# A first product that waits for two PSUM banks: a hybrid RWKV-7 and Conformer backbone on one core

## The chip, the core and the metric

The kernel runs on one NeuronCore of a Trainium2 chip. The metric is the device time in microseconds of one execution, the median of several runs. The engines meant below are TensorE (PE, with its weight loads as PEld), VectorE (DVE), ScalarE (ACT), GpSimd (POOL) and SyncE (SP), each with an instruction stream of its own. TensorE writes its products to PSUM banks of 128 x 512 fp32; ScalarE and VectorE read them from there.

## The reference, cut to what matters

A backbone of two layers over 512 latent tokens with a prefix of 256 context tokens and a width of 1024. The first layer runs a bidirectional RWKV-7 time mixing (16 heads of 64) beside a gated short convolution; the second is a Conformer convolution module. The change lies in the time mixing, whose core is this recurrence, run forwards and backwards:

```python
def wkv_scan(S0, r, decay, k, v, kk, a, reverse):
    def step(S, inp):
        r_t, w_t, k_t, v_t, kk_t, a_t = inp
        sa = jnp.einsum("bhvk,bhk->bhv", S, -kk_t)
        S = (S * w_t[:, :, None, :]
             + sa[..., None] * (kk_t * a_t)[:, :, None, :]
             + v_t[..., None] * k_t[:, :, None, :])
        return S, jnp.einsum("bhvk,bhk->bhv", S, r_t)
    S, out = lax.scan(step, S0, (r, decay, k, v, kk, a), reverse=reverse)
    return out, S
```

All of it is fp32. The context is scanned first from a zero state, and its final states start the scan of the latent tokens.

## The kernel before

The scan is done in chunks of 64 tokens, for one pair of heads (128 channels, 64 partitions for each head) at a time: 4 blocks of context (`c0` to `c3`), then 8 latent pairs, each of 8 chunks and two directions `z`. For each pair there are these steps, in functions of their own:

- `light0` and `lightz` (one call for each direction) make the decays and the scaled keys and queries, `AR` and `BK`. Each call of `lightz` makes two small dense products, `lw` and `la`, that ScalarE reads with a Tanh (lines 511 and 517).
- `heavy` makes what the recurrence needs from each chunk. For a latent pair its parts run in the order `A`, `N`, `B`, `V`. `pa` (A) forms the head products in four groups, each half of the chunks of one direction: 4 chunks times 2 heads, so 8 products of 64 rows, the heads on the two halves of the partitions. Head `h` writes to a bank of its own, `pas[h]`, and VectorE reads both with a masked multiplication into `E` (line 601), first head 0, then head 1. `pb` (B) transposes the keys in two groups, one for each direction, of 16 small transposes (line 576) into two banks `pbs[h]`, which ScalarE copies into `BKt` (line 612).
- `solve` inverts the small triangular systems on VectorE (lines 656 and 658), `merge` joins their blocks, and `chain_lat` runs the recurrence, chunk by chunk.

All these banks come from one tag, `at`, with two buffers. A product may write to a bank once the reader of what stood there before is done. In the code of `pa` and `pb` the products of a group alternate between the banks, head 1 first. `pinned()` returns a helper that ties each product of a group to the one before it, so that their order on TensorE is the written one.

What stands between the products of a group is left to a planner. It fixes the order of each engine's instructions when the program is built: among those whose inputs and buffers it expects to be ready, it takes the earliest by the written order, with some tied to later points by hand (`HEAVY_AFTER`, `CONV_AFTER`, `issue_after`). While the small products of a pair wait, it issues the dense products of 128 x 512 of the convolution branch and the gates (`pcg`, `pxb`, `pbg`, `pzb`, each 24 instructions, from `conv_branch`).

The stages of the latent pairs follow each other in the order of `STAGE[1]`: recurrence of pair s, then bonus product, solve for pair s + 1, loads and light part of pair s + 2, merge for pair s + 1, heavy part of pair s + 2, fills and finish, convolution branch. After the last pair come the output projection and the Conformer layer.

Of the kernel before, what the change touches and what calls it, by code (L numbers as in the profile page):

```python
# [10 lines left out]
AF = mybir.ActivationFunctionType  # L11
ALU = mybir.AluOpType
# [3 lines left out]
P = 128  # L16
# [6 lines left out]
CH = 64  # L23
NCTX = CTX // CH
NLAT = SEQ // CH
# [12 lines left out]
ZR = (slice(0, 64), slice(64, 128))  # L38
# [13 lines left out]
def kernel(ctx: ExitStack, tc: tile.TileContext, I: dict, out: bass.AP):  # L52
    nc = tc.nc
    V, S, G, T = nc.vector, nc.scalar, nc.gpsimd, nc.tensor
# [122 lines left out]
    def w(tag, name, dt=F32):  # L177
        return wk.tile([P, SIZE.get(tag, 512)], dt, tag=tag, name=name, bufs=NBUF.get(tag, 1))

    def ch3(t, x=CH):  # L180
        return t.rearrange("p (c x) -> p c x", x=x)

    def small(name, shape):
        return cvp.tile(shape, F32, tag=name, name=name)
# [7 lines left out]
    maskE = small("maskE", [P, 3, P])  # L192
    scm = small("scm", [P, NLAT * 66])
    sg = small("sg", [P, NLAT, 66])
# [12 lines left out]
    def hc(nmh, j):  # L207
        return hcol[:, half[nmh] + j : half[nmh] + j + 1]
# [297 lines left out]
    def lightz(st, z):  # L506
        lat, nm, parts, low, kk = (st[x] for x in ("lat", "nm", "parts", "low", "kk"))
        k_, r_, bon = st["k"], st.get("r"), st.get("bon")
        pl = low(0, z, f"lw{nm}{z}")
        for p, cs in parts:  # L510
            S.activation(sg[:, cs.start // CH : cs.stop // CH, 1:65], ch3(pl[:, cs]), AF.Tanh,
                         bias=hc("w0", z * 8 + p), scale=0.5)
        S.activation(sg[:, :, 1:65], sg[:, :, 1:65], AF.Identity, bias=ones)
        pl = low(1, z, f"la{nm}{z}")
        a = w("a", f"a{nm}{z}")
        for p, cs in parts:
            S.activation(a[:, cs], pl[:, cs], AF.Tanh, bias=hc("a0", z * 8 + p), scale=0.5)
        cumf = w("P", f"P{nm}{z}")
        cum = ch3(cumf, 66)
        sgf = sg.rearrange("p c x -> p (c x)")  # L520
        V.tensor_tensor_scan(cumf, scm, sgf if z == 0 else sgf[:, ::-1], 0.0, ALU.mult, ALU.add)
        iP = ch3(w("tmp", f"iP{nm}{z}"))
        S.activation(iP, cum[:, :, 1:65], AF.Exp, scale=0.5 * KAPPA)
        S.activation(cumf, cumf, AF.Exp, scale=-0.5 * KAPPA)
        PC = w(f"PC{z}", f"PC{nm}{z}")
        S.copy(PC, cum[:, :, 64])
        st["PC"].append(PC)
        kd = w("kd", f"kd{nm}{z}")
        for p, cs in parts:
            S.activation(kd[:, cs], a[:, cs], AF.Identity, scale=hka[:, p : p + 1], bias=oka[:, p : p + 1])  # L530
        V.tensor_tensor(out=kd, in0=kd, in1=k_, op=ALU.mult)
        if lat:
            p = st["p"]
            rk = col("r_k", 8 * z + p)
            if z:
                V.scalar_tensor_tensor(out=bon, in0=kd, scalar=rk, in1=bon, op0=ALU.mult, op1=ALU.add)
                V.tensor_tensor(out=bon, in0=bon, in1=r_, op=ALU.mult)
            else:
                S.activation(bon, kd, AF.Copy, scale=rk)
        V.scalar_tensor_tensor(out=a, in0=a, scalar=1.0, in1=kk, op0=ALU.add, op1=ALU.mult)  # L540
        AR = ch3(w("AR", f"AR{nm}{z}"), P)
        BK = ch3(w("BK", f"BK{nm}{z}"), 3 * CH)
        kka, ba, kdc, Pr, iPr = ch3(kk), ch3(a), ch3(kd), cum, iP
        if z:
            Pr, iPr = Pr[:, ::-1, :], iP[:, ::-1, :]
            kka, ba = kka[:, :, ::-1], ba[:, :, ::-1]
        if not lat:
            V.scalar_tensor_tensor(out=AR[:, :, 0:CH], in0=kka, scalar=-1.0, in1=Pr[:, :, 0:CH],
                                   op0=ALU.mult, op1=ALU.mult)
        else:  # L550
            V.scalar_tensor_tensor(out=AR[:, :, 0:CH], in0=kka, scalar=-1.0, in1=Pr[:, :, 0:CH],
                                   op0=ALU.mult, op1=ALU.mult)
            Pi = Pr[:, :, 1:65]
            V.tensor_tensor(out=AR[:, :, CH:], in0=ch3(r_), in1=Pi[:, :, ::-1] if z else Pi, op=ALU.mult)
        V.scalar_tensor_tensor(out=BK[:, :, ZR[1]], in0=ba, scalar=0.5, in1=iPr, op0=ALU.mult, op1=ALU.mult)
        V.tensor_tensor(out=BK[:, :, ZR[0]], in0=kdc, in1=iPr[:, :, ::-1] if z else iPr, op=ALU.mult)
        S.copy(BK[ZR[1], :, P:], BK[ZR[1], :, ZR[0]])
        st["AR"].append(AR)
        st["BK"].append(BK)

    def pinned():
        prev = []

        def go(o, lhsT, rhs, start=True, stop=True, op=mm):
            e = op(o, lhsT, rhs, start, stop)
            if prev:
                tc.add_manual_dep(e.ins, prev[-1].name,
                                  mybir.DependencyInfo(mybir.DependencyClass.NoSync, mybir.DependencyReason.DATA),
                                  reason="written order")
            prev[:] = [e.ins]  # L570
            return e

        return go
# [7 lines left out]
    def heavy(st, an=None):  # L581
        ha = (None,) * 4 if an is None else HEAVY_AFTER[an["lat"]]
        lat, nm = st["lat"], st["nm"]
        v_ = st["v"]
        UV = buf("UV", st)
        E = buf("E", st)
        st["UV"], st["E"], st["BKt"] = UV, E, [buf("BKt", st, z) for z in range(2)]

        def pa():
            for gi, (z, g) in enumerate(PA_ORDER if lat else ((0, 0), (1, 0))):  # L590
                with anchored(an, ha[gi if lat else 2 * gi]):
                    AR, BK = st["AR"][z], st["BK"][z]
                    m, x = (4, P) if lat else (8, CH)
                    c0 = m * g
                    pas = [ch3(ps_at(f"pa{nm}{z}{g}{h}"), x) for h in range(2)]
                    go = pinned()
                    for c in range(m):
                        for h in (1, 0):
                            go(pas[h][:, c, :], kb(BK, h, c0 + c), AR[ZR[h], c0 + c, 0:x])
                    for h in range(2):  # L600
                        V.tensor_tensor(out=E[:, h, z * NLAT + c0 : z * NLAT + c0 + m, :], in0=pas[h],  # L601
                                        in1=maskE[:, z * (1 + h) : z * (1 + h) + 1, 0:x].to_broadcast([P, m, x]), op=ALU.mult)

        def pb():
            for z in range(2):
                pbs = [ch3(ps_at(f"pb{nm}{z}{h}")) for h in range(2)]
                go = pinned()
                for c in range(NLAT):
                    for h in (1, 0):
                        go(pbs[h][:, c, :], kb(st["BK"][z], h, c), ident[ZR[h], ZR[h]], op=tr)  # L610
                for h in range(2):
                    S.copy(st["BKt"][z][:, :, ZR[h]], pbs[h])

        def nt():
            for h in range(2):
                for b in range(2):
                    rs = slice(64 * (1 - h) + 32 * b, 64 * (1 - h) + 32 * b + 32)
                    S.copy(Nt[rs], E[rs, h, :, 32 * b : 32 * b + 32])

        def pv():  # L620
            pv = ch3(ps_at(f"pv{nm}"))
            for c in range(NLAT):
                for h in range(2):
                    mm(pv[ZR[h], c, :], v_[ZR[h], c * CH : (c + 1) * CH], ctr[ZR[h], ZR[h]], True, True)
            for z in range(2):
                for h in range(2):
                    src = pv[ZR[h]].rearrange("p (j c) x -> p j c x", j=2)
                    dst = UV[ZR[h], z * NLAT : (z + 1) * NLAT, ZR[h]].rearrange("p (j c) x -> p j c x", j=2)
                    S.copy(dst, src if lat or not z else src[:, :, ::-1, :])

        def po():
            if lat:
                bon = st["bon"]
                pb = ps_at("pbon" + nm)
                mm(pb, blk, bon, True, True)
                V.scalar_tensor_tensor(out=bon, in0=pb, scalar=0.5, in1=v_, op0=ALU.mult, op1=ALU.mult)

        st["po"] = po
        for x in HEAVY[lat]:
            {"A": pa, "B": pb, "N": nt, "V": pv, "O": po}[x]()  # L640
# [278 lines left out]
    for s in range(12):  # L919
        st = sts[s]  # L920
# [9 lines left out]
        for x in STAGE[s >= 4]:  # L930
# [17 lines left out]
            elif x == "C":  # L948
                conv_branch(s - 3, st["anchor"])
                if s == 10:  # L950
                    rs.close()
                    op = rs.enter_context(tc.tile_pool(name="op", bufs=1, reuse_waits="tile", side="right"))
# [40 lines left out]
    with ExitStack() as l1:  # L993
# [118 lines left out]
        for n in range(4):  # L1112
            ws = {}
            for part, tag in ((1, "wa"), (0, "wb")):
                for kt in range(0, KT, 2):
                    c0 = part * EC + n * 512
# [6 lines left out]
            for m in range(4):  # L1123
# [10 lines left out]
                a = lt("a", f"a{n}{m}")  # L1134
# [31 lines left out]
        for j in range(16):  # L1166
            c0 = 2 * EC + j * P
# [138 lines left out]
```

## Time and profile before

| | us |
|---|---|
| median of three runs | 1466.74 |
| lowest and highest run | 1463.91, 1472.64 |
| span of the profiled execution | 1468.7 |
| TensorE busy in it | 1417.8 |
| VectorE busy | 987.8 |
| ScalarE busy | 749.9 |
| GpSimd busy | 128.4 |

The span is counted from the first to the last instruction of one execution that the profiler recorded; no other time is given for that execution. In the timeline a row gives the start and the length of an instruction, or of several of a kind that follow each other (x14), with the idle time before it and what ended it in brackets. Matmul lengths overlap, as they are pipelined, so distances from start to start are what counts. An fp32 product of the heads is two instructions, a transpose is one; a group of `pa` thus shows as 16 instructions `pal<-ARl,BKl` and a group of `pb` as 16 instructions `pbl<-ident,BKl`. The granted clock of TensorE was 0.978 of full speed on average over the span.

### The profile page before, as it was taken

Reading aid. Unit: us, or ns where it says so; the run is one execution under the profiler, and the core shown is the slowest. Engines: PE = TensorE matmul, PEld = TensorE weight load, DVE = VectorE, ACT = ScalarE, POOL = GpSimd, SP = SyncE. Lnnn points to the kernel's source line nnn. Section 1 sums busy time; section 2 is a strip of 40 time slices with the busy share of each in tenths; the row PEclk is TensorE's granted clock in tenths of the full one; section 3 lists DMA queues with packets and bytes.
Section 4 is the critical chain, followed back from the end, with each engine's and each line's share of the span. In section 5 each row is a group of like instructions: output and inputs, shape, how many; then the busy total and the mean of one; then the engine's idle time right before and its main releaser. Section 6 shows DMA issues by size and latency. Waiting matters only on the chain. (4 is left out here: it accounts for less than half of the span.)

```text
span 1468.7 us, 29754 instructions
## 1 busy us (share of the span) xinstructions
PE 1417.8 (97%) x11921; PEld 1014.3 (69%) x11921; DVE 987.8 (67%) x2298; ACT 749.9 (51%) x1516; POOL 128.4 (9%) x250
## 2 busy tenths in 40 slices
PE   6999999999999999999999999999989999999998
PEld 1564677878776766666666666777757777788876
DVE  2675587567798989898998988558535535544333
ACT  4536364353655575666656655447543423463222
POOL 2023210000110101101011000011100000000000
PEclk9999999979898999999999999999999999999999
DMA  9755433312232312222222222468503303123322
GB/s 318 221 169 165 151 112 94 99 40 76 75 91 80 97 54 87 64 80 66 68 86 77 61 68 70 169 227 295 177 16 115 104 12 115 58 88 100 100 87 86
DMA packets 137627, 158.55 MB, mean 108 GB/s; under 512 B 15375, under 2 KB 104143, under 8 KB 137369
## 3 DMA queue, kind: packets, MB, share of 16 engines
q1 hardware_dynamic: 121104, 106.47, 23.1%
q0 software_dynamic: 15312, 48.99, 10.2%
q8 instruction: 94, 1.54, 0.4%
q10 hardware_dynamic: 1072, 1.19, 0.3%
q14 instruction: 45, 0.37, 0.1%
HBM read 138.33 MB, written 18.28 MB: 107 GB/s over the span
## 5 line engine op out<-in xcount | busy, mean ns | idle before, releaser
L57 PE MATMUL o<-wh,y 128*128 128x512 f32 x248 | 80.5, 402 | 0.0
L656 DVE TENSOR_TENSOR xtmpl<-Xl,Yl 128x126 f32<-128x126 f32 (+22 forms) x248 | 62.1, 251 | 2.9
L658 DVE TENSOR_TENSOR Yl<-Yl,xtmpl 128x126 f32<-128x126 f32 (+22 forms) x248 | 62.0, 250 | 2.6
L57 PE MATMUL pal<-ARl,BKl 64*128 64x128 f32 x512 | 57.2, 301 | 3.5 <-DVE xtmpc L656 2.1
L57 PEld LDWEIGHTS pal<-ARl,BKl 64*128 64x128 f32 x512 | 42.1, 190 | 23.0 <-issue 5.4
L1141 ACT CAST ah<-a 64x512 fp32r<-64x512 f32 x32 | 19.8, 618 | 72.9 <-DVE a L1136 72.5
L57 PE MATMUL zol<-UV,E 64*64 64x64 f32 (+1 forms) x1024 | 54.0, 221 | 0.0
L57 PE MATMUL o<-wl,y 128*128 128x512 f32 x124 | 50.0, 403 | 4.0 <-DVE wl L127 4.0
L57 PEld LDWEIGHTS o<-wh,y 128*128 128x128 f32 x248 | 46.6, 191 | 10.1 <-ACT wh L126 0.2
L764 ACT COPY UV<-uh 64x128 f32<-64x128 f32 x128 | 33.3, 260 | 39.7 <-PE uh L57 32.1
L127 DVE TENSOR_TENSOR wl<-wr,wh 128x1024 fp32r<-128x1024 f32 x28 | 37.0, 1320 | 22.0 <-ACT wh L126 21.8
L57 PE MATMUL zol<-Hl,ARl 64*64 64x64 f32 x896 | 50.2, 230 | 0.2
L57 PEld LDWEIGHTS zol<-Hl,ARl 64*64 64x64 f32 x896 | 35.0, 133 | 19.9 <-issue 16.2
L1136 DVE TENSOR_TENSOR a<-pu,a 128x512 f32<-128x512 f32 x16 | 11.0, 690 | 51.3 <-PE pu L57 49.0
L57 PEld LDWEIGHTS uh<-UV,BKt 128*64 128x64 f32 x704 | 26.3, 137 | 27.1 <-ACT UV L764 21.4
L1097 DVE SCALAR_TENSOR_TENSOR pr<-px,dbe,What 119x512 f32<-119x512 f32 x32 | 22.5, 746 | 32.5 <-PE px L57 32.4
L601 DVE TENSOR_TENSOR E<-pal,maskE 128x512 f32<-128x512 f32 x64 | 42.9, 684 | 1.7 <-PE pal L57 1.4
L57 PEld LDWEIGHTS zol<-UV,E 64*64 64x64 f32 (+1 forms) x1024 | 42.3, 136 | 2.5 <-ACT UV L764 1.9
L771 DVE SCALAR_TENSOR_TENSOR Hl<-uh,PCl,HPl 128x64 f32<-128x64 f32 x112 | 26.5, 277 | 25.7 <-PE uh L57 15.9
L126 ACT CAST wh<-wr 128x1024 fp32r<-128x1024 f32 x28 | 29.4, 1049 | 22.4 <-DMA wr<-in_ev_w_out_dram 13.0
L57 PE MATMUL uh<-UV,BKt 128*64 128x64 f32 x704 | 36.3, 232 | 1.9 <-ACT UV L764 1.8
L57 PEld LDWEIGHTS uh<-Ol,E 64*64 64x64 f32 x512 | 19.9, 133 | 22.8 <-ACT Ol L758 12.7
(941 smaller groups left out, 4292.8 us busy)
## 6 DMA issues: line engine op xcount, KB each, us to landing
wr<-in_ev_w_out_dram SPq DMA_DIRECT2D x28, 512.0 KB, 5.2
mwo<-in_mod_w_dram POOLq DMA_DIRECT2D x28, 256.0 KB, 3.3
mwr<-in_mod_w_dram POOLq DMA_DIRECT2D x28, 256.0 KB, 4.1
ectx<-in_mod_w_dram SPq DMA_DIRECT2D x12, 512.0 KB, 4.6
wrk<-in_ev_w_in_dram SPq DMA_DIRECT2D x16, 256.0 KB, 3.0
wrv<-in_ev_w_in_dram SPq DMA_DIRECT2D x16, 256.0 KB, 4.2
wrr<-in_ev_w_in_dram SPq DMA_DIRECT2D x16, 256.0 KB, 2.8
wrza<-in_ev_w_in_dram SPq DMA_DIRECT2D x16, 256.0 KB, 2.9
```

The source lines that it names most:

```text
L57: return T.matmul(o, lhsT, rhs, start=start, stop=stop)
L126: S.copy(hi, raw)
L127: env["lo"].tensor_tensor(out=lo, in0=raw, in1=hi, op=ALU.subtract)
L601: V.tensor_tensor(out=E[:, h, z * NLAT + c0 : z * NLAT + c0 + m, :], in0=pas[h], in1=maskE[:, z * (1 + h) : z * (1 + h) + 1, 0:x].to_broad ...
L656: V.tensor_tensor(out=tv, in0=X[:, :i, i : i + 1].to_broadcast([P, i, m]), in1=Y[:, i : i + 1, c0:].to_broadcast([P, i, m]), op=ALU.mult)
L658: V.tensor_tensor(out=Y[:, :i, c0:], in0=Y[:, :i, c0:], in1=tv, op=ALU.add)
L764: u_ = S.copy(UV[ZR[1 - h], i : 2 * nch - i : 2 * nch - 1 - 2 * i, ZR[h]], uh[ZR[1 - h], 0:2, :])
L771: h_ = V.scalar_tensor_tensor(out=Hn[:, z, :], in0=uh[:, 2 + z, :], scalar=PC[z][:, i : i + 1], in1=HP[:, z, :], op0=ALU.mult, op1=ALU.add)
L1097: V.scalar_tensor_tensor(out=pr[s][:NPROD], in0=px[s][:NPROD], scalar=dbe[:, 0:1], in1=What[:, n * 512 : n * 512 + 512], op0=ALU.add, op1= ...
L1136: V.tensor_tensor(out=a, in0=pp[1], in1=a, op=ALU.mult)
L1141: S.copy(ahl[s][hr], a[hr])
```

## The change

The first product of each latent group gets a dependence on the readers of the two banks used last: for the first group of a pair the readers of `lw` and `la` of the second direction, for each later group the two readers of the group before. The lists are kept in `st["ev"]`. Groups of the context blocks get none. No operation is added or taken away, and no size or buffer changes.

```diff
@@ lightz
         pl = low(0, z, f"lw{nm}{z}")
+        st["ev"] = []
         for p, cs in parts:
-            S.activation(sg[:, cs.start // CH : cs.stop // CH, 1:65], ch3(pl[:, cs]), AF.Tanh,
-                         bias=hc("w0", z * 8 + p), scale=0.5)
+            e_ = S.activation(sg[:, cs.start // CH : cs.stop // CH, 1:65], ch3(pl[:, cs]), AF.Tanh,
+                              bias=hc("w0", z * 8 + p), scale=0.5)
+            st["ev"].append(e_)
...
-            S.activation(a[:, cs], pl[:, cs], AF.Tanh, bias=hc("a0", z * 8 + p), scale=0.5)
+            st["ev"].append(S.activation(a[:, cs], pl[:, cs], AF.Tanh, bias=hc("a0", z * 8 + p), scale=0.5))
@@ pinned
-    def pinned():
+    def pinned(behind=()):
         prev = []
 
         def go(o, lhsT, rhs, start=True, stop=True, op=mm):
             e = op(o, lhsT, rhs, start, stop)
+            if not prev:
+                for x in behind:
+                    tc.add_manual_dep(e.ins, x.ins.name,
+                                      mybir.DependencyInfo(mybir.DependencyClass.Sync, mybir.DependencyReason.DATA),
+                                      reason="both banks free")
@@ heavy, pa
-                    go = pinned()
+                    go = pinned(st["ev"] if lat else ())
+                    st["ev"] = []
...
-                        V.tensor_tensor(out=E[:, h, z * NLAT + c0 : z * NLAT + c0 + m, :], in0=pas[h],
-                                        in1=maskE[:, z * (1 + h) : z * (1 + h) + 1, 0:x].to_broadcast([P, m, x]), op=ALU.mult)
+                        st["ev"].append(V.tensor_tensor(
+                            out=E[:, h, z * NLAT + c0 : z * NLAT + c0 + m, :], in0=pas[h],
+                            in1=maskE[:, z * (1 + h) : z * (1 + h) + 1, 0:x].to_broadcast([P, m, x]), op=ALU.mult))
@@ heavy, pb
-                go = pinned()
+                go = pinned(st["ev"] if lat else ())
+                st["ev"] = []
...
-                    S.copy(st["BKt"][z][:, :, ZR[h]], pbs[h])
+                    st["ev"].append(S.copy(st["BKt"][z][:, :, ZR[h]], pbs[h]))
```

## The prediction

> **What bounds the kernel now.** I read the head of the page, then the busy time by stretches, then TensorE's timeline in the stretch where the change acts.
>
> ```profile
> span 1468.7 us, 29754 instructions
> ...
> 430.00:900.00 470.00, 459.66 (x5764) 316.44 (x5764) 424.79 (x1203) 292.87 (x671) 49.44 (x89) 0.99 0.25 75
> ```
>
> The columns of the second row are stretch, length, and busy time of PE, PEld, DVE, ACT and POOL. All latent head pairs lie in this stretch: TensorE is busy for 459.66 of 470 us (98%), VectorE for 424.79 (90%). TensorE sets the pace, with VectorE close behind, so a saving on TensorE counts until VectorE is late. The next two views show one group of head products (`pal`, 8 products, two instructions each) between dense products of the gate projection `pbg`: first TensorE (start, length), then VectorE.
>
> ```profile
> 625.75 0.39 PE L57 MATMUL pbg<-hlh,whbg 128*128 128x512 f32 x1
> 625.98 0.40 PE L57 MATMUL pbg<-hll,whbg 128*128 128x512 f32 x1
> 626.30 0.48 PE L57 MATMUL pal<-ARl,BKl 64*128 64x128 f32 x2
> 626.72 0.50 PE L57 MATMUL pbg<-hlh,wlbg 128*128 128x512 f32 x1
> 627.06 0.40 PE L57 MATMUL pbg<-hlh,whbg 128*128 128x512 f32 x1
> 627.38 1.16 PE L57 MATMUL pal<-ARl,BKl 64*128 64x128 f32 x14
> 628.47 0.50 PE L57 MATMUL pbg<-hll,whbg 128*128 128x512 f32 x1
> ```
>
> ```profile
> 625.08 0.69 DVE L601 TENSOR_TENSOR E<-pal,maskE 128x512 f32<-128x512 f32 x1 [0.32 <-PE pal L57]
> 625.84 0.69 DVE L601 TENSOR_TENSOR E<-pal,maskE 128x512 f32<-128x512 f32 x1
> 569.29 1.16 PE L57 MATMUL pal<-ARl,BKl 64*128 64x128 f32 x14 [0.29 <-DVE E L601]
> ```
>
> The group is cut. Its first product (x2) goes at 626.30, after the first bank of the previous group has been read (625.08 + 0.69 = 625.77) and before the second has (625.84 + 0.69 = 626.53). Two dense products follow, then the other seven (x14). The row at 569.29 is a group in which no dense product stood between: the seven waited for the second reader by themselves. So the first product claims whichever bank is free first, and the second product is the one that needs the other bank. That is the wait which the change moves forward.
>
> **The change, part by part.** It adds no instruction. It adds dependences of the first product of 48 latent groups (8 pairs, 4 groups of head products and 2 of key transposes each) on both readers of the two banks before. Where both readers are on one engine, in order, the later one is what is waited for, and the group's second product waits for that reader today. Nothing of a group can end later through the wait itself, and queued behind the waiting product are only the group's own products and whatever the planner puts behind them. What goes is the cut.
>
> *A cut in a group of head products.* Start to start, from the rows above, the cut version takes 0.32 (dense to small), 0.42 (the lone product), 0.34 (the first dense after it), 0.32 (dense to small), 1.09 (the seven): 2.49 us. Uncut it would be two dense products at 0.23 (625.75 to 625.98) as the last becomes 0.32, so 0.23 + 0.23 + 0.32, and the eight. What eight take instead of seven is shown by a group cut elsewhere:
>
> ```profile
> 515.76 0.71 PE L57 MATMUL pal<-ARl,BKl 64*128 64x128 f32 x6
> 516.40 1.20 PE L57 MATMUL uh<-aml,E 32*32 32x32 f32 x64
> 517.53 0.71 PE L57 MATMUL pal<-ARl,BKl 64*128 64x128 f32 x8
> 518.17 0.50 PE L57 MATMUL pzb<-hlh,wlzb 128*128 128x512 f32 x1
> ```
>
> Three products take 0.64 us and four take 0.64: the two heads of a chunk run side by side, and the head that lost its partner costs a place of its own. So eight take the 1.09 of seven, uncut is 1.87 us, and a cut costs 2.49 - 1.87 = 0.62 us.
>
> *A cut in a group of transposes* (`pbl`, 16 instructions). The first two rows are an uncut group, the others a cut one.
>
> ```profile
> 520.43 0.71 PE L576 MATMUL pbl<-ident,BKl 64*128 64x64 f32 x16
> 521.08 0.50 PE L57 MATMUL pzb<-hlh,whzb 128*128 128x512 f32 x1
> ...
> 756.88 0.27 PE L576 MATMUL pbl<-ident,BKl 64*128 64x64 f32 x1
> 757.08 0.50 PE L57 MATMUL pzb<-hlh,wlzb 128*128 128x512 f32 x1
> ...
> 757.97 0.71 PE L576 MATMUL pbl<-ident,BKl 64*128 64x64 f32 x15
> 758.61 0.50 PE L57 MATMUL pzb<-hlh,wlzb 128*128 128x512 f32 x1
> ```
>
> The lone transpose takes 0.20, the fifteen 0.64, the sixteen 0.65. With the two extra changes of shape (0.32 and 0.34 in place of 0.23 each) a cut costs 0.20 + 0.64 - 0.65 + 0.09 + 0.11 = 0.39 us.
>
> *How many.* I counted the lone first products in the timeline; the first and the last of each kind:
>
> ```profile
> 439.03 0.48 PE L57 MATMUL pal<-ARl,BKl 64*128 64x128 f32 x2
> 871.77 0.49 PE L57 MATMUL pal<-ARl,BKl 64*128 64x128 f32 x2
> ...
> 462.32 0.27 PE L576 MATMUL pbl<-ident,BKl 64*128 64x64 f32 x1
> 879.96 0.27 PE L576 MATMUL pbl<-ident,BKl 64*128 64x64 f32 x1 [0.16 <-ACT BKt L612]
> ```
>
> Head products: 24 (2 in pair 0, 4 in pair 1, 3 in each of pairs 2 to 7). Two of them, one each in pairs 2 and 3, have no dense product in between; they stood waiting and I count them as 0. The first one (439.03) I count as 0 too: the next group waits 2.14 us for VectorE (row at 446.57 below), so TensorE would only wait longer. That leaves 21 x 0.62 = 13.0 us. Transposes: 15 x 0.39 = 5.9 us. Together **18.9 us** of TensorE time, by pair 1.4, 2.87, 2.02, 2.02 and four times 2.64. The first groups of pairs 2 to 7 lie in pieces between the steps of the recurrence; the change there is worth 6 x 0.62 = 3.7 us at most, or as much the other way if a chain step falls behind the unbroken group. I take 0.
>
> *What is late next.* The saving falls into the stretch of each pair where VectorE is busiest, since it reads the banks, solves for the next pair and splits weights there. The rows are for pairs 1 to 7, 30 us each.
>
> ```profile
> 500.00:530.00 30.00, 29.60 (x378) 21.77 (x377) 25.48 (x50) 17.40 (x35) 2.75 (x5) 1.00 0.33 100
> 560.00:590.00 30.00, 27.83 (x362) 19.67 (x360) 29.01 (x79) 15.90 (x28) 4.58 (x8) 1.00 0.31 95
> 620.00:650.00 30.00, 29.11 (x376) 20.42 (x377) 28.48 (x78) 16.93 (x30) 4.20 (x8) 1.00 0.30 90
> 680.00:710.00 30.00, 29.31 (x370) 20.66 (x366) 28.36 (x75) 16.79 (x30) 3.96 (x8) 1.00 0.29 89
> 740.00:770.00 30.00, 29.41 (x385) 20.36 (x384) 27.04 (x70) 17.18 (x32) 3.61 (x7) 1.00 0.28 81
> 800.00:830.00 30.00, 30.00 (x386) 20.67 (x380) 27.48 (x71) 17.36 (x32) 3.88 (x7) 1.00 0.26 81
> 860.00:890.00 30.00, 29.84 (x401) 21.38 (x402) 27.49 (x68) 17.01 (x32) 1.62 (x3) 1.00 0.27 81
> ```
>
> VectorE's idle time there is 4.5, 1.0, 1.5, 1.6, 3.0, 2.5 and 2.5 us. A stretch cannot shrink by more than that while VectorE's work stays in it. Upper bound, the smaller of saving and idle time: 1.4 + 2.87 + 0.99 + 1.52 + 1.64 + 2.64 + 2.52 + 2.51 = 16.1 us. Lower bound, if only half of the idle time can be closed (the rest being the time from a product to its reader): 1.4 + 2.26 + 0.5 + 0.76 + 0.82 + 1.48 + 1.26 + 1.26 = 9.7 us. I take the middle, **12.9 us**, since TensorE hardly idles in pairs 5 to 7, which speaks for the upper bound, while pairs 2 to 4 already stand on VectorE, which speaks for the lower. From the profiled span that is 1468.7 - 12.9 = 1455.8; the span lies 2.0 above the median of 1466.74, so the median becomes 1466.7 - 12.9 = 1453.8, about 1454.
>
> **The rivals.**
>
> *Everything is passed on.* The planner fills the time freed with dense products and VectorE's work spreads out: 18.9 us, and up to 3.7 from the first groups, so 1444 to 1448; I set 1447. For it: pairs 5 to 7 hardly wait. Against it: pairs 2 to 4.
>
> *VectorE keeps its order and its pace.* Then only the two pairs with ample idle time gain, 1.4 + 2.87 = 4.3 us: 1462. For it: 29.01 of 30 us busy in pair 2. Against it: pair 6, where TensorE is busy for 30.00 of 30.
>
> *It does not do what it says.* The planner starts the first product only when both banks are free already, and cuts for another reason: 1466.7. Against it: the order 625.77, 626.30, 626.53 above, which is the cut by banks; for it, that some first products start after both readers on the chip.
>
> *Slower by the clock.* The freed time gathers in front of one VectorE result per pair instead of being spread. A long wait already happens once:
>
> ```profile
> 446.57 1.75 PE L57 MATMUL pal<-ARl,BKl 64*128 64x128 f32 x16 [2.14 <-DVE xtmpc L656]
> 450.00:460.00 10.00, 9.87 (x167) 8.13 (x167) 6.82 (x12) 2.04 (x6) 0.54 (x1) 0.55 0.37 113
> ```
>
> After 2.14 us of waiting the next whole slice ran at a granted clock of 0.55 (the column after the busy times), so 10 us did the work of 5.5 and 4.5 us were lost. Shorter waits did not do it: in 560 to 590 TensorE idled for 2.17 us in pieces and the clock stayed at 1.00. If a pair's whole 2.6 us becomes one wait, that pair loses its gain and 4.5 us on top, 7.1 in all; from three such pairs on (21.3 against 18.9) the kernel is slower, and with four it stands at 1466.7 - 18.9 + 28.4 = 1476. Against it: the banks are read at several points per pair, each with dense products to hand. The Trainium skill, "TensorE: Matmul & The Clock Gate", "What's actually happening", speaks for a milder form: the clock falls after an idle window of about 3.4 us. By that page a wait of 2.6 us would cost itself alone, and four such pairs would leave a gain of some 8 us, an estimate; the rows above show the fall after 2.14 us, so I keep the price from the rows.
>
> *Slower by the banks.* Between the first bank's release and the second's, another product could now take the first bank.
>
> ```profile
> 531.61 0.54 POOL L408 DMA_DIRECT2D vl<-psp  x1 [3.96 <-DVE bonl L636]
> DMA to landing us min/median/max: 2.9/3.0/3.3
> 535.43 0.69 ACT L517 ACTIVATE al<-lal,hcol 128x512 f32<-128x512 f32 x1
> 543.83 0.49 PE L57 MATMUL lwl<-tanhl,lwhl 128*128 128x512 f32 x1
> 577.11 0.97 PE L57 MATMUL pvl<-ctr,vl 64*64 64x64 f32 x26
> ```
>
> Against it: `vl` had landed by 535, both banks were empty from 536.1 to 543.8, and `pvl` still waited until 577 for its turn in the written order. If it happened, the group's second product would wait for one more product and its reader, about 2 x 0.4 + 0.69 = 1.5 us by the rows of a dense instruction and of a reader, and the group would stay cut. Twice in each of seven pairs that is 14 x 1.5 = 21 us, with 14 x 0.62 = 8.7 of the 18.9 us not gained: 1466.7 + 21 - 10.2 = 1477.
>
> **How the numbers follow.** Chances: forecast 0.44, all passed on 0.14, VectorE's pace 0.20, no effect 0.07, clock 0.09, banks 0.06. About 0.5% (7.3 us) is what a measurement of this kernel can tell from no change. Faster by more than that: the forecast and all passed on, 0.58. Within it: VectorE's pace and no effect, 0.27. Slower: clock and banks, 0.15. The forecast's own range is 1450 to 1457, from the two bounds. The range for 8 in 10 leaves out the two slower cases and the far end of "all passed on": 1446 to 1469.
>
> **What would show it.** Right: lone first products (x2 of `pal`, x1 of `pbl`) fall from 39 to a few; groups stand as x16; the pairs' period shrinks by 1 to 2.6 us; TensorE's busy time falls by some 15 to 19 us. Wrong: the busy time falls but waits for `E`, `aml`, `Ol` or `BKt` rise by the same (VectorE's pace); lone first products remain (no effect); a slice with a granted clock near 0.55 in a pair that had 1.00 (clock); `pvl`, `pbonl` or `ssl` between two groups (banks). A planner that reorders more than the groups would spoil the sum without any of these.

## The result

The changed kernel takes 1467.94 us (median of 20 runs, 1459.86 to 1474.49), the kernel before 1471.41 in the same series (20 runs, 1463.91 to 1480.08). The medians lie 3.5 us apart. The ratio is 0.997 with a 95% interval of 0.9956 to 0.9984: some 4.4 us less, where 12.9 were forecast. The profiled execution of the changed kernel is one of its fastest, 1459.91 us for a span of 1458.1.

### The profile page after: what moved, and what is told of

It reads as the page before. It is cut to its first block, busy times and chain, and to the rows that moved or that the text cites. A ratio compares the mean times of both kernels' runs of the same rounds, so it can differ in the third digit from the quotient of the medians.

```text
span 1458.1 us, 29782 instructions
## 1 busy us (share of the span) xinstructions
PE 1394.8 (96%) x11921; PEld 1004.5 (69%) x11921; DVE 987.0 (68%) x2298; ACT 751.1 (52%) x1516; POOL 128.8 (9%) x250
## 3 DMA queue, kind: packets, MB, share of 16 engines
q0 software_dynamic: 15312, 48.99, 10.6%
## 4 chain that ended last, share of the span: by engine, by line
PE 70%; DVE 14%; ACT 6%; DMA 5%; issue 4%; POOL 0%; SPq 0%; DVEq 0%; ACTq 0%; POOLq 0%
PE pu L57 13%; PE f L57 6%; PE pz L57 6%; PE uh L57 5%; PE zol L57 4%; PE pcg L57 3%; PE plk L57 3%; PE plv L57 3%; PE pxb L57 3%; PE pza L57 3%; DVE E L609 2%; PE plr L57 2%; PE o L57 2%; PE zoc L57 2%; PE pcv L57 2%
## 5 line engine op out<-in xcount | busy, mean ns | idle before, releaser
L57 PE MATMUL pal<-ARl,BKl 64*128 64x128 f32 x512 | 45.8, 300 | 7.9 <-DVE E L609 3.7
L57 PEld LDWEIGHTS pal<-ARl,BKl 64*128 64x128 f32 x512 | 36.3, 194 | 18.6 <-issue 7.8
```

Source lines behind the costliest of these rows:

```text
L57: return T.matmul(o, lhsT, rhs, start=start, stop=stop)
```

## The profile after

Head of the page of the changed kernel, its row for the head products (busy us, mean ns, idle before), and its busy time by stretches as in the prediction (length, then PE, PEld, DVE, ACT, POOL, granted clock). The five short stretches are those of pairs 3 to 7, set at the same distance from the next start of the recurrence as the prediction's.

```profile
span 1458.1 us, 29782 instructions
PE 1394.8 (96%) x11921; PEld 1004.5 (69%) x11921; DVE 987.0 (68%) x2298; ACT 751.1 (52%) x1516; POOL 128.8 (9%) x250
...
L57 PE MATMUL pal<-ARl,BKl 64*128 64x128 f32 x512 | 45.8, 300 | 7.9 <-DVE E L609 3.7
```

```profile
430.00:900.00 470.00, 446.11 (x5876) 314.25 (x5876) 425.82 (x1210) 293.30 (x678) 49.20 (x89) 0.98 0.26 75
...
613.10:643.10 30.00, 27.93 (x389) 20.80 (x389) 28.51 (x81) 16.98 (x31) 4.58 (x8) 1.00 0.28 81
672.30:702.30 30.00, 27.48 (x373) 20.47 (x372) 28.63 (x78) 16.91 (x30) 3.64 (x7) 1.00 0.34 96
731.70:761.70 30.00, 27.70 (x402) 20.50 (x398) 27.86 (x73) 17.69 (x33) 3.65 (x7) 1.00 0.30 89
791.20:821.20 30.00, 28.44 (x388) 20.34 (x387) 27.55 (x72) 17.46 (x33) 3.89 (x7) 1.00 0.30 86
850.70:880.70 30.00, 28.34 (x389) 21.01 (x390) 28.00 (x70) 16.96 (x32) 1.62 (x3) 1.00 0.27 81
```

TensorE is busy for 23 us less (1417.8 to 1394.8), of which some 6 belong to a slow spell in the profile of before (shown below), and the span is not 23 us shorter. In the five stretches TensorE's idle time rises from 2.3 us in all to 10.1 (five times 30 less the busy times), and VectorE's falls from 11.2 only to 9.5. Of the 39 lone first products none is left. Not every group is whole: apart from the first groups of pairs 2 to 7, which still lie between the steps of the recurrence, five groups of head products and three of transposes are cut further on by the merge's `uh`. From TensorE's timeline of the changed kernel (start, length):

```profile
618.00 1.16 PE L57 MATMUL pal<-ARl,BKl 64*128 64x128 f32 x16
...
752.56 0.71 PE L583 MATMUL pbl<-ident,BKl 64*128 64x64 f32 x16 [0.29 <-ACT BKt L622]
```

What took the cuts' place shows in TensorE's waits in the 470 us from 430 on (in all, times, longest), before and then after; these are the longest of each.

```profile
PE pal L57 <- DVE xtmpc L656: 2.1, 1, 2.1
PE uh L57 <- ACT UV L764: 1.8, 4, 0.7
PE uh L57 <- DVE aml L665: 1.4, 2, 0.9
PE pbl L576 <- ACT BKt L612: 1.3, 5, 0.4
PE pal L57 <- DVE E L601: 1.3, 3, 0.8
```

```profile
PE pal L57 <- DVE E L609: 3.7, 4, 2.2
PE uh L57 <- DVE aml L675: 3.5, 5, 1.2
PE pal L57 <- DVE Yc L668: 3.4, 1, 3.4
PE pbl L583 <- ACT BKt L622: 3.2, 6, 0.9
PE uh L57 <- ACT UV L774: 1.8, 6, 0.7
PE pbl L583 <- DVE E L609: 1.7, 4, 0.8
```

The readers of the banks (`E`, `BKt`) and the merge (`aml`) now end last, 19 times in the eight pairs. The pace itself is read from the first product of each recurrence, those of pairs 1 and 6, before and then after:

```profile
585.10 0.45 PE L57 MATMUL zol<-h,ARl 64*64 64x64 f32 x8
...
886.46 0.45 PE L57 MATMUL zol<-h,ARl 64*64 64x64 f32 x8
```

```profile
579.92 0.45 PE L57 MATMUL zol<-h,ARl 64*64 64x64 f32 x8
...
877.19 0.45 PE L57 MATMUL zol<-h,ARl 64*64 64x64 f32 x8
```

The group stretches of pairs 3 to 7 lie between the two: 301.36 us before, 297.27 after, so **4.1 us** arrive, where 8.2 were forecast for these pairs (the middle of 5.6 and 10.8) out of 12.6 us of TensorE time (2.02 and four times 2.64). From pair to pair it is 1.7, 0.8, 0.6, 0.5 and 0.5. Busy time between these starts, before and then after, the clock at 1.00 in both:

```profile
585.10:886.46 301.36, 297.64 (x3926) 202.30 (x3925) 273.68 (x799) 189.05 (x447) 30.15 (x54) 1.00 0.24 72
```

```profile
579.92:877.19 297.27, 284.96 (x3926) 199.07 (x3925) 272.97 (x797) 189.82 (x446) 30.21 (x54) 1.00 0.25 74
```

TensorE's idle time rises from 3.7 to 12.3 us, by 8.6, and 4.1 + 8.6 = 12.7. So the time was saved as forecast, and two thirds of it stand as waits.

The two profiled spans differ by 10.6 us, more than the medians. About half of it, 5.4 us, is there ahead of the first changed group already (439.03 and 433.66), after a slow spell in the profile of before alone. The same rows by stretches, before and then after:

```profile
380.00:400.00 20.00, 18.54 (x245) 15.08 (x244) 12.21 (x20) 10.07 (x19) 1.67 (x3) 0.68 0.29 81
```

```profile
380.00:400.00 20.00, 18.27 (x306) 14.38 (x304) 16.22 (x27) 13.79 (x28) 2.21 (x4) 1.00 0.27 81
```

A granted clock of 0.68 for 20 us costs up to 6.4 us. The rest is -0.2 us from the first changed group to the recurrence of pair 1, the 4.1 us, and 1.3 us after the recurrence of pair 6 has begun, where no group of the change stands. What the change did in the profile is thus 3.9 us.

## The experiments

The theories in what follows: **P**, VectorE's work sets the pace and gives TensorE's saving back as waits; **O**, the planner's new order is worse; **F**, the cut lay where TensorE would wait for a reader anyway, by latency and not by volume of work. Two later ones sharpen P and F: **S**, VectorE's chain of results in its fixed order ends last once the cuts are gone; **L**, latencies bind, whichever engine reads. Ratios are against the kernel before in the same series, with 95% intervals.

### One part of the change alone

The dependences for the head products alone (`pa_only`), for the transposes alone (`pb_only`):

```diff
 # pa_only, in pb():
-                go = pinned(st["ev"] if lat else ())
+                go = pinned()
 # pb_only, in pa():
-                    go = pinned(st["ev"] if lat else ())
+                    go = pinned()
```

> The dependences on the groups of head products alone (32 of the 48 groups). Theory P (VectorE's work sets the pace): its part of the gain, 13.0 of 18.9, so some 3 us faster than the kernel before. Theory F (a cut lay where TensorE would have waited for a reader anyway, because the planned order has too few dense products ahead of the group): nearly all of the gain, 3 to 4.5 us, since the waits in front of the transposes took back 4.9 of their 5.9 us.

Measured: 1467.91, ratio 0.9973 (0.9958 to 0.9988).

> The dependences on the groups of transposes alone (16 groups, 15 cuts of 0.39 us). Theory P: 1 to 2 us faster than the kernel before. Theory F: 0 to 1.5 us, with waits for BKt and E in front of the groups of 3 to 5 us in all.

Measured: 1472.32, ratio 1.0014 (0.9995 to 1.0032). As far as these intervals tell, the whole gain is the head products'. The transposes' 5.9 us do not arrive: with their cuts alone gone, TensorE's waits for `aml`, `BKt` and `Ol` stand at 2.5, 2.3 and 2.3 us, 7.1 in all, where the kernel before has 1.4, 1.3 and 1.0.

### Less work for VectorE

The second half of the split weights of four projections is left out (64 instructions of 0.69 us; VectorE's records overlap, and its busy time falls by some 0.34 us for each).

```diff
 def w_half(src, name):
     raw = wp.tile([P, 512], F32, tag="wr", name="wr" + name, bufs=2)
+    if name[:2] in ("cg", "xb", "bg", "zb"):
+        hi = wp.tile([P, 512], F32R, tag="wh", name=f"wh{name}", bufs=3)
+        nc.sync.dma_start(raw.rearrange("p (k c) -> p k c", c=src.shape[2]), src)
+        S.copy(hi, raw)
+        return hi, hi
```

> The kernel before, with the subtraction for the low half of the convolution branch's weights left out and the high half used in its place: 64 VectorE operations of 0.69 us fewer, 44 us, and the same products on TensorE. Theory P (VectorE sets the pace of the stretch with the groups, so what TensorE saves there comes back as waits): the cuts keep TensorE busy for 98% here, so the time falls by 0 to 8 us, the idle time of TensorE between 430 and 900 us being 10 us. Theory O (the new dependences make the planner put things in a worse order, whatever VectorE's load): the same here, 0 to 8 us.

Measured: 1471.74, ratio 0.9999 (0.9977 to 1.0021).

> The changed kernel with the same subtraction left out. Theory P: with VectorE relieved the 14 to 18 us of TensorE time that the change takes away are passed on, so this is 10 to 18 us faster than b_light, and TensorE's waits for E, aml and Ol fall back to about 2 us in all. Theory O: it is 3 to 5 us faster than b_light, as the changed kernel is against the kernel before.

Measured: 1465.75, ratio 0.995 (0.9929 to 0.997). VectorE's busy time is 22 us shorter (page: 987.8 to 966.1, and 987.0 to 965.0). In the kernel before that is worth nothing that can be measured, in the changed one 2 to 3 us, with an interval that overlaps the changed kernel's own, so that even this is not shown. The lead is 6 us, short of the 10 that P asked for and over the 5 of O. Nor do the waits fall back to the 2 us in all that P asked for: those for `E` and `aml` stand at 3.6 and 1.2 us, and those for `Hl` rise to 3.2.

The same subtraction moved to GpSimd (`env["lo"] = G` for these four weights):

> The kernel before with the same subtraction done by GpSimd in place of VectorE (half of the 2.6 us that 128x1024 takes there, so about 1.3 us each); nothing is left out. Theory P: 0 to 6 us faster than the kernel before, as b_light, less what the longer way to a weight's low half costs. Theory O: the same.

Measured: 1533.51, ratio 1.0416 (1.0384 to 1.0449).

> The changed kernel with that subtraction on GpSimd. Theory P: 8 to 16 us faster than b_pool, and with it the fastest correct kernel so far, 1453 to 1460 where the kernel before takes 1470. Theory O: 3 to 5 us faster than b_pool.

Measured: 1516.9, ratio 1.0297 (1.0267 to 1.0327). A miss as a way to relieve VectorE: the row of `wlbg` on GpSimd shows 1716 ns each, against 685 ns on VectorE in the kernel before, and the recurrence waits for `Hl` on VectorE (11.8 us in both).

### More work for VectorE

The same 64 subtractions done twice:

```diff
-        return hilo(src, raw, hi, lo)
+        hilo(src, raw, hi, lo)
+        if name[:2] in ("cg", "xb", "bg", "zb"):
+            V.tensor_tensor(out=lo, in0=raw, in1=hi, op=ALU.subtract)
+        return hi, lo
```

> The kernel before, with the low-half subtraction of the conv-branch weights (cg, xb, bg, zb) done twice on VectorE: 64 more VectorE instructions, some 22 us more of its work (what the light variants took away), the output unchanged. P (VectorE's stream takes back what TensorE saves): the kernel before has cover for part of it, so it slows by less than the changed kernel does, to 1472 to 1480. F (the group products' waits are latencies, not volume): 1471 to 1475, and the changed kernel keeps its lead of some 4 us.

Measured: 1505.88, ratio 1.0236 (1.0206 to 1.0266).

> The changed kernel with the same 64 VectorE instructions more. P: the lead over the kernel before goes: within 1.5 us of the heavy kernel before. F: the lead stays, 3 to 6 us under the heavy kernel before.

Measured: 1495.29, ratio 1.016 (1.0136 to 1.0184). Some 32 us of VectorE's busy time more (page: 987.8 to 1020.2, and 987.0 to 1019.0) cost 34 and some 27 us. Both theories had far too little here, and P has the wrong sign: the lead does not go, it grows to 10.6 us. Much of all this passes through the clock: its mean is 0.960 in the runs of the heavy kernel before and 0.965 in those of the heavy changed one, where the kernel before beside them has 0.977 (median). By these figures, as an estimate, some 25 of the 34 us are clock (0.017 of 1500 us), and 7 to 8 of the 10.6 us of the lead (0.005 of 1500 us). TensorE's waits and three short stretches of the heavy changed kernel show how it comes about:

```profile
PE pal L57 <- DVE E L612: 28.0, 19, 5.8
```

```profile
625.00:630.00 5.00, 2.45 (x24) 1.72 (x22) 5.00 (x16) 2.08 (x4) 2.37 (x4) 1.00 0.31 97
630.00:635.00 5.00, 2.84 (x32) 2.65 (x32) 5.00 (x18) 0.62 (x1) 0.00 (x0) 0.70 0.02 5
635.00:640.00 5.00, 5.00 (x30) 3.48 (x29) 4.63 (x20) 3.04 (x6) 0.00 (x0) 0.62 0.36 105
```

TensorE stands for about half of ten microseconds, VectorE is busy throughout, and the clock falls to 0.70 and 0.62, which costs another 3.4 us (5 x 0.30 + 5 x 0.38). So more work for VectorE than it has here costs about its own length, and less of it brings next to nothing.

### Another order on ScalarE, and more dense products ahead of the waits

`a_abnv` writes the transposes' copies ahead of the copies into `Nt`.

```diff
-HEAVY = ("VBOAN", "ANBV")
+HEAVY = ("VBOAN", "ABNV")
```

> The changed kernel with the transposes ahead of the copies for the solve in the written order of a latent pair, so that ScalarE reads the transposes' banks before its four copies of 0.62 us. Theory F: the waits for BKt (3.2 us) go, and up to 3 us are gained. Theory P: VectorE gets the solve's input 1 to 2 us later in each pair, so no gain, or up to 8 us slower.

Measured: 1468.22, ratio 0.9973 (0.9956 to 0.9991). The planner did not take the order up, as ScalarE's timeline of this kernel shows:

```profile
815.80 2.51 ACT L628 COPY Nt<-E 32x512 f32<-32x512 f32 x4 [1.92 <-DVE E L609]
818.33 1.07 ACT L622 COPY BKt<-pbl 128x512 f32<-128x512 f32 x2
```

`Nt` still goes first, here and in all pairs but one, so this run says nothing of the order.

`a_fill` ties the first product of groups or merges behind one to five further dense products, where the changed kernel had waited, at 14 places (its expectation counts 13):

```diff
+FILL_AT = {2: {'m': ('zb', 22)}, 3: {'b0': ('zb', 16), 'm': ('zb', 17)}, 4: {'m': ('bg', 22), 'b1': ('zb', 8)},
...
+    def fill_order(p):
+        for what, (name, k) in FILL_AT.get(p, {}).items():
+            tc.add_manual_dep(firsts[p, what].ins, dense_[p - 1, name][k].ins.name,
+                              mybir.DependencyInfo(mybir.DependencyClass.NoSync, mybir.DependencyReason.DATA),
+                              reason="behind a dense product")
```

> The changed kernel with 13 further orderings, without any wait on another engine: in pairs 2 to 7 the first product of some groups, and the first product of the merge, stand behind a given dense product of bg or zb, 1 to 5 further on than in the changed kernel. Those dense products run now behind the waits, before the next recurrence. Theory F: the waits at these places (about 6 us) fall by 4 or more and the time by 3 to 6 us against the changed kernel. Theory P: VectorE's results come no earlier, the waits only move to later places, and the time is within 1.5 us of the changed kernel.

Measured: 1465.94, ratio 0.9966 (0.9951 to 0.9981). TensorE's waits in this kernel:

```profile
PE pal L58 <- DVE E L626: 4.3, 5, 2.3
...
PE zol L58 <- DVE Hl L802: 2.5, 4, 0.9
...
PE po L58 <- DVE Ol L835: 2.1, 3, 1.1
PE pbl L598 <- ACT BKt L641: 1.3, 3, 0.5
...
PE uh L58 <- DVE aml L694: 1.1, 2, 0.8
```

The waits that were filled fell (`BKt` 3.2 to 1.3, `aml` 3.5 to 1.1), and others rose (`Hl` 0.7 to 2.5, `Ol` 1.2 to 2.1). The waits move; their sum does not go: in the 470 us TensorE is idle for 23.9 us in the changed kernel and for 24.1 here.

`al_fill` has both the lighter VectorE and the orderings, `pa_fill` the orderings on `pa_only`.

> The changed kernel with both remedies: the low-half subtraction of the conv-branch weights left out (the high half is used in its place, so the output is coarser) and the 13 orderings that put dense products ahead of waiting ones. If VectorE's volume and the planned order share the blame, the two add up: 1465.75 less some 2 us, or more, 1455 to 1463. If what binds is the chain from one recurrence to the next, which neither shortens, 1464 to 1467 like each alone.

Measured: 1466.45, ratio 0.9959 (0.994 to 0.9978): the two do not add up.

> The added waits for the head products alone, none for the transposes, with the same 13 orderings. If the transposes' wait costs what it saves, as the split of the change said: 1465 to 1467, like the changed kernel with the orderings. If it costs more than it saves once the other waits are filled: 1462 to 1464, and this is the best of the correct kernels.

Measured: 1466.21, ratio 0.9958 (0.994 to 0.9975): like `a_fill`. The interval is not apart from that of the changed kernel, so no version that computes the whole reference is shown to beat it.

### Readers off VectorE, and other work out of their way

The chain of waits of the changed kernel (start, length, where the time went) ran like this in one group stretch, which gave theory S:

```profile
674.13 0.60 DVE E L609
...
677.24 0.59 DVE wlbg L127
...
679.46 0.66 DVE yb L851
...
681.83 0.60 DVE E L609
...
684.72 0.63 DVE aml L675
...
691.01 0.96 ACT BKt L622 x2
692.01 0.72 PE pbl L583 x16
...
695.86 3.63 PE pzb L57 x15
699.49 0.55 PE zol L57 x13
```

For 12 us VectorE goes from one result to the next, and what stands between two readers of banks is other work of the pair. The last two rows are the end of the stretch: fifteen dense products, and the next recurrence. `split` moves the second reader of each latent group of head products to ScalarE, `defer` moves the two `yb` instructions behind the merge's `Pml`:

```diff
 # split (in before the same without the list)
-                        st["ev"].append(V.tensor_tensor(
-                            out=E[:, h, z * NLAT + c0 : z * NLAT + c0 + m, :], in0=pas[h],
+                        out = E[:, h, z * NLAT + c0 : z * NLAT + c0 + m, :]
+                        st["ev"].append(S.activation(out, pas[h], AF.Tanh, scale=0.001) if lat and h else V.tensor_tensor(
+                            out=out, in0=pas[h],
 # defer, in conv_branch(), for both instructions e; late is Pml
...
+            tc.add_manual_dep(e.ins, late.ins.name,
+                              mybir.DependencyInfo(mybir.DependencyClass.NoSync, mybir.DependencyReason.DATA),
+                              reason="behind the merge")
```

> The kernel before, where the second of the two readers of each latent head-product group moves from VectorE to ScalarE (some 4 reads of 0.6 to 0.7 us in each of 8 pairs, some 20 us of VectorE's work in the group stretches, and the two readers of a group run side by side). What it leaves out: ScalarE cannot multiply by the mask, so that half is squashed by a tanh of a thousandth of it instead, and the output is not the reference's. S (in the group stretch VectorE's in-order chain is what ends last once TensorE has its cuts back): before, TensorE itself fills that stretch, so 1463 to 1471. L (latencies bind, whatever engine reads): 1467 to 1472.

Measured: 1469.13, ratio 0.999 (0.997 to 1.0011).

> The changed kernel with the same move of the second readers to ScalarE; the same is left out. S: the lead over the kernel before so altered grows from 4 us to 9 us or more. L: it stays within 3 to 6 us.

Measured: 1466.87, ratio 0.9976 (0.9956 to 0.9997).

> The kernel before, with two VectorE instructions of each pair's convolution branch (the two accumulations into yb, some 0.66 us each) put behind the merge's last VectorE copy (Pml) in VectorE's order, so out of the group stretch's chain; nothing is left out. S: TensorE fills the stretch before, so no gain: 1469 to 1474. L: the same.

Measured: 1476.36, ratio 1.0032 (1.0007 to 1.0056).

> The changed kernel with the same two instructions put behind Pml. S: up to 1.3 us a pair in 6 to 7 pairs, 4 to 9 us under the changed kernel: 1459 to 1464. L: 1466 to 1469, as the changed kernel.

Measured: 1471.67, ratio 1.0006 (0.9986 to 1.0025). The leads are 2.3 us with the split, where S asked for 9, and 4.7 with the deferral, where the changed kernel became slower, not faster, and the kernel before more so (some 4 us of that by its mean clock, 0.975 against 0.978 in the kernel before beside it): S falls. L had the first lead too large and the second kernel too fast, so it is not borne out in its numbers either. In `a_split` TensorE's timeline shows what remained, in the stretch of pair 4:

```profile
684.70 1.16 PE L57 MATMUL pal<-ARl,BKl 64*128 64x128 f32 x16 [0.57 <-DVE orq L425]
...
687.60 0.62 PE L57 MATMUL po<-ident,Ol 64*64 64x64 f32 x13 [0.84 <-DVE Ol L815]
```

It waits twice there, while dense products are left over for the end of the stretch. `a_split_fill` puts 3 to 7 of them ahead of these two waits in pairs 4 to 7 (`FILL_AT` for the fourth group and for `po`):

> The changed kernel with the second readers of the latent head products on ScalarE (their half squashed by a tanh instead of masked, as in the split kernels) and with 8 orderings that put 3 to 7 more dense products ahead of the fourth group and of the transposes of the pair before, in the four pairs where the split kernel waited 0.6 to 1.0 us at each of the two while 16 dense products were left over for the end of the stretch. If the written order is what keeps the saving from arriving once the readers are quicker: some 1.5 us a pair, 5 to 7 us under the split kernel, 1459 to 1462. If the waits only move on: 1465 to 1468.

Measured: 1464.13, ratio 0.9949 (0.993 to 0.9967), between the two expectations. It is the lowest median of all, 8 us under the kernel before; but its interval overlaps that of `a_split`, so that order and quicker readers add up is not shown. The mean clock is 0.981 here and 0.978 in the kernel before beside it, which by the fit given below is worth some 4 of the 8 us; whether the shorter waits caused that or chance did, no run tells. Most of the saving still does not arrive.

### TensorE time taken from the kernel before in another way

The last gate, `zb`, is projected with two products of a row block instead of three (`two` is true for it alone).

```diff
-    def proj(wt, o, h):
+    def proj(wt, o, h, two=False):
         for kt in range(KT):
             ks = slice(kt % 4 * P, kt % 4 * P + P)
             wh, wl = wt[kt // 4]
+            if two:
+                mm(o, wh[:, ks], h[0][:, kt, :], kt == 0, False)
+                mm(o, wl[:, ks], h[0][:, kt, :], False, kt == KT - 1)
+                continue
             mm3(o, wh[:, ks], wl[:, ks], h[0][:, kt, :], h[1][:, kt, :], kt == 0, kt == KT - 1)
...
-        proj(wt, pz, hlat)
+        proj(wt, pz, hlat, nm == "zb")
```

> The kernel before without one of the three products of each row block of the last gate of the convolution branch (the low half of the input against the high half of the weights; left out, so the output is coarser): 64 dense products fewer, eight in each of the eight pairs, 0.23 us from start to start where they stand dense at the end of a group stretch, so some 14.8 us of TensorE time less by another way than the cuts, with every VectorE and ScalarE instruction kept. If TensorE's time sets the end before: 10 to 15 us less, 1456 to 1461. If what sets it is the chain of readers and merge beside TensorE: 0 to 6 us less, 1465 to 1471.

Measured: 1467.92, ratio 0.9989 (0.9971 to 1.0007): some 1.6 us for 14.8 us of TensorE time (4.2 between the medians). This run needs neither groups nor readers touched, and its profile shows the same exchange: first the stretch from 430 to 900 and one of 5 us, then the longest waits, then TensorE's timeline.

```profile
430.00:900.00 470.00, 451.89 (x5725) 313.11 (x5727) 422.60 (x1210) 293.27 (x675) 49.32 (x90) 0.97 0.26 75
...
570.00:575.00 5.00, 5.00 (x19) 3.35 (x16) 4.60 (x19) 2.46 (x4) 0.00 (x0) 0.50 0.37 105
```

```profile
PE pal L57 <- DVE E L605: 5.4, 8, 1.5
PE uh L57 <- DVE aml L669: 3.6, 5, 1.1
```

```profile
568.28 0.48 PE L57 MATMUL pal<-ARl,BKl 64*128 64x128 f32 x2 [1.52 <-DVE E L605]
569.07 2.07 PE L57 MATMUL pal<-ARl,BKl 64*128 64x128 f32 x14 [0.31 <-DVE E L605]
```

TensorE's idle time in the 470 us goes from 10.3 to 18.1 us, in waits for `E` (1.3 to 5.4) and `aml` (1.4 to 3.6). As much again is lost to the clock: a wait of 1.52 us and one of 0.31 are followed by 5 us at half clock, in which seven head products take 2.07 us instead of 1.16. With a second such spell at 862 us the clock takes 8.5 us in this stretch that it does not take in the kernel before (3.4 by the three rows of 5 us from 565 on, 5.1 by those from 860 on). Over its 12 runs the mean granted clock is 0.973, against 0.978 in the 23 of the kernel before beside it. In those 23 the time rises by 1.2 us for each 0.001 of clock that is missing, so some 5.5 us of the 14.8 went that way, by this estimate. The run therefore lies between its two expectations: without the clock's share some 7 of the 14.8 us would have arrived.

## Why the prediction was wrong, step by step

- **The cuts.** Right: the lone first products are gone, and eight products have the length of 1.16 us that seven had.
- **Price and number of cuts.** Right in size: 12.7 us of 12.6 in pairs 3 to 7. In pairs 0 to 2, where 4.7 of the 12.9 us were to come, nothing arrived in the profile: from the first changed group to the recurrence of pair 1 it is 146.07 us before and 146.26 after. TensorE's idle time there rose from 6.6 to 11.5 us. The first wait alone grew from 2.1 us for `xtmpc` to 3.4 for `Yc`, which the prediction had counted as 0. The mean granted clock there fell from 0.96 to 0.94, some 3 us.
- **"What is late next": the step that failed.** The saving was bounded by VectorE's idle time, half to all of it. Of the 11.2 us in the five stretches only 1.7 were closed, and the gain of 4.1 us lies under the lower bound of 5.6 for them. In its place TensorE waits 8.6 us more: 4.8 of them for `E`, `BKt` and `aml`, the rest in small pieces, most of it for other results of VectorE (`Pml`, `wlbg`, `Hl`). That VectorE is idle does not say that it could start its next instruction earlier; the prediction did not look at what each idle piece waited for.
- **"TensorE sets the pace, so a saving on TensorE counts until VectorE is late".** This premise of the step fails in the kernel before already: 14.8 us less for TensorE gave 1.6 (`b_less`), and waits and a lower clock took the rest. A saving counts only where TensorE does not spend it waiting for a result further on in its own order.
- **The rivals.** "VectorE keeps its order and its pace" had the time right (4.3 us) and the sign for it, waits for `E`, `aml` and `BKt` in place of the busy time. It had the place wrong: it gave the gain to pairs 0 and 1, and 0.5 to 1.7 us came from each of pairs 3 to 7. Its reason, VectorE's volume, is not borne out: 22 us less on it brought at most 2 to 3 us. "All passed on" and "no effect" are out by the rows above. So is "banks": in the changed kernel's trace no `pvl`, `pbonl` or `ssl` stands between the groups of a pair. "The clock" happened once more than before, in pair 2 of the changed kernel, in TensorE's timeline and the row of the stretch after it:

```profile
563.30 1.16 PE L57 MATMUL pal<-ARl,BKl 64*128 64x128 f32 x16 [2.25 <-DVE E L609]
...
565.00:570.00 5.00, 5.00 (x30) 3.40 (x31) 4.46 (x20) 3.98 (x7) 0.00 (x0) 0.69 0.36 105
```

It cost some 1.6 us (5 x 0.31), and the mean clock is 0.978 in the 20 runs of the changed kernel and in 35 of the kernel before (the series of `pa_only`), so it does not carry the result.

One thing the traces of both kernels show and the prediction did not use: ahead of each recurrence of pairs 1 to 6 TensorE runs without a gap for 2.4 us or more, and the last thing there is 3 to 17 dense products (15 in the chain above). So the recurrence starts when TensorE's fixed order comes to it. A wait further up in this order delays it, although dense products stand behind the wait; moving some of them ahead (`a_fill`) moved the waits.

What stays open is why the awaited results come no earlier, and so what sets the pair's period of 59 to 60 us. It is not VectorE's volume (`light`), not the readers' engine (`split`) and not the written order (`fill`), each taken alone, and not TensorE's own work alone (`b_less`, half of whose miss is clock); readers and order together stand at 8 us under the kernel before, some 4 of them by the clock. The recurrence's own steps, which take about 35 of the 60 us (585.10 to the last `zol` of its pair at 620.3 in the kernel before), were changed by no run.

## What to carry to other kernels

An engine busy for 98% need not pass on what you save on it: in a fixed order the saving can come back as a wait for another engine, and the wait as a lower clock. Take some of its work away first, as `b_less` does, and see how far the time follows, before you price savings on it. Idle time of the next engine is no measure of what it can take up; look at what each of its idle pieces waits for. And a stall that is moved behind cover costs nothing only while there is cover left: fill one wait with dense products, and the next one lacks them.

## What the runs showed of the hardware

- The granted clock fell after shorter waits than the prediction priced: after 1.52 and 0.31 us (`b_less`, 0.50 in the next 5 us). The Trainium skill, "TensorE: Matmul & The Clock Gate", "What's actually happening", names an idle window of about 3.4 us ahead of the fall; these rows do not agree.
- Such spells differ from run to run of one kernel and go with most of the spread: among the 20 runs of the changed kernel the shortest, 1459.86 us, had a mean clock of 0.983, the longest, 1474.49 us, one of 0.972, and over all 20 the correlation of time and clock is -0.89.
- The response to VectorE's work is one-sided: 22 us less changed the kernel before by nothing that can be measured, and 32 us more by 34, most of it by a clock of 0.960 in place of 0.977.
